# A single-core kernel: the first modulation is loaded first, split into high and low parts, and the preparation of the convolution is moved behind it

## The chip, the core and the metric

The kernel runs on one core of one Trainium2 chip. The metric is the time of one execution on the device in microseconds, lower is better. The median of three runs of the kernel before is 4174.78 us.

## The reference

Two blocks of a sequence model over 1024 tokens of width 1024, batch 1, in float32. What matters here is the start of the first block:

```python
def rmsnorm(x, g):
    xf = x.astype(jnp.float32)
    y = xf * lax.rsqrt(jnp.mean(xf * xf, axis=-1, keepdims=True) + EPS)
    return y.astype(x.dtype) * g

def modulation(cond, w_mod, b_mod):
    m = jax.nn.silu(cond) @ w_mod + b_mod
    return jnp.split(m, 3, axis=-1)
...
    shift, scale, gate = modulation(c[:, None, :], w_mod[i], b_mod[i])
    h = rmsnorm(x, norm_g[i]) * (1 + scale) + shift
    cshift, cscale, cgate = modulation(c_ctx[None, None, :], w_mod[i], b_mod[i])
    hc = rmsnorm(ctx, norm_g[i]) * (1 + cscale) + cshift
    a_val, a_gate, q, k, v, b_gate = jnp.split(h @ w_in, EVEN_SPLITS, axis=-1)
```

`c` and `c_ctx` are two condition vectors of 1024 values, `w_mod[0]` is 1024 x 3072, `ctx` has 256 tokens. Attention, pooling, a second layer with a long convolution (Hyena), Fourier mixing, and then an S5 layer, a stick-breaking attention and two feed-forward layers follow. The long convolution works with spectra of filters that depend on the weights alone: a small sine network over 1024 positions gives hidden units, these give the taps, and the taps are normalized and Fourier transformed. That is the "convolution's preparation" here; its results are not needed before the second layer of the first block.

## The kernel before

Tokens lie along the free dimension and channels on the 128 partitions, in tiles of 128 x 1024 float32 (512 KB, 4 KB on each partition). Large products are made of pairs of tiles in the fp32r type: a high part (a cast on ScalarE) and a low part (the rest, a subtraction on VectorE), with three matmuls for high x high, high x low and low x high (`mm3`, lines 202 to 204; `split`, lines 215 and 216; `weights`, lines 179 to 185, for a panel of weights). Nearly all working tiles come from one pool of 40 slots of 4 KB per partition (`t` and `tr`, tag "t"); weight panels have two slots for the arriving matrix ("wt") and four for its two parts ("wq"); PSUM has two buffers of 1024 columns (`psB`) and four of 512 (`psb`).

The code writes the instructions in one order, and the framework's planner places them into one queue for each engine, by their written order and by when it reckons their operands and slots to be there; an instruction that is free early can so come ahead of what is written before it. On the chip each queue runs in its placed order, and semaphores make an instruction wait for its operands and for its slot. SyncE (SP) issues nearly all loads, GpSimd (POOL) the stores and some copies.

`build` works in this order. `load_consts` loads small constants. `K.hy = Work(K.hy_prep(), 0.6)` makes the preparation of the convolution a generator; a step of it runs up to the next `yield`. `ev_norm` makes the first norm: it runs one step of the preparation, loads x (8 tiles, line 350), runs four more steps (hidden units of the filters, `hy_filters`; tables and the first weights), squares x on ScalarE and sums the squares on VectorE (`sq_acc`, lines 239 to 243), does the same for ctx (`xc`, line 359), and calls `modulation0`.

`modulation0` takes the first 2048 columns of `w_mod[0]` in 16 tiles of 512 KB (`wm`, line 276). Each tile is multiplied in plain float32: the stationary operand is 128 x 2 (the two conditions, `silu_c`), the moving operand half a tile, 512 columns (line 278). After each tile two steps of the preparation are written, 32 in all, so 37 with the five of `ev_norm`. The two rows of results are copied from PSUM (`mrow`, line 285), turned into columns by 16 small matmuls (`pm`, line 288), and give `gain0` and `shift0` (lines 290 to 297). Then `rms_half` makes h in two halves of 512 tokens: column sums (`pc`, line 220), the power -0.5 on GpSimd (`rs_r`, line 228), a broadcast by matmul (`pr`, line 233), and for each of eight tiles one VectorE instruction (`nt`, line 258), the high part on ScalarE (`hh`, line 261) and the low part on VectorE (`hl`, line 262). The same follows for ctx.

`ev_in` is the large input projection: 18 panels of the weights `w_ev` against h (`pbg` gates, `pav`, `pag`, `pq`, `pk`, `pv`); the first two gate panels share the halves, so that they start on the first half of h. Each step over k in `gemm` calls `go()`, 344 calls in all, and `go` issues `rate` steps of the preparation behind each (0.6, that is 206 steps), and 0.1 steps of the other modulations.

The preparation has 5 steps for the hidden units and tables, and 12 spectra of 19 steps: 233. A spectrum (`hy_spectrum`) has 16 matmuls for taps (`pf`, lines 896 and 897), VectorE and ScalarE work on them, a sum over partitions (`pl`, line 918), a row (`pl1r`, line 929), 64 small matmuls as recorded for the transform (`pk`, lines 947 and 948), and 8-point transforms on VectorE, whose results go to DRAM (`khat`, line 955).

Of the kernel before, what the change touches and what calls it, by code (L numbers as in the profile page):

```python
# [35 lines left out]
        ("ln_mix_g_2", 16), ("ln_mix_b_2", 16), ("ln_ffn_g_2", 16), ("ln_ffn_b_2", 16), ("cond", 16))  # L36
# [8 lines left out]
class Work:  # L45
    """instructions that are issued between others, `rate` steps behind each step of a product"""
# [15 lines left out]
class Norm:  # L62
    """layer norm to a (hi, lo) tile per half, and to DRAM; st: the tiles and their sums, set by their product;
    keep: the float32 result replaces the tiles"""
# [39 lines left out]
class Core:  # L104
# [27 lines left out]
    def with_work(self, gen, fg, rate):  # L132
        """runs fg with gen between its products, then the rest of gen"""
        w = Work(gen, rate)
        self.work.insert(0, w)
        fg()
        w.drain()
        self.work.remove(w)

    def lagged(self, tasks):  # L140
        """(product, use) pairs: each use is issued behind the next product"""
# [33 lines left out]
    def weights(self, src, shape, big=False):  # L175
        """a panel of weights as (hi, lo) tiles"""
# [11 lines left out]
    def first4(self, srcs, acts):  # L188
        """four panels, the first half of all before the second; acts: tiles and columns of each half"""
# [55 lines left out]
    def rms_half(self, xs, acc, hv, gain, shift, outs, n=HB):  # L245
        """generator"""
# [19 lines left out]
    def modulation0(self):  # L266
        """shift and scale of block 0, for both conditions"""
# [3 lines left out]
        mod = self.c("mod0", [P, 16, 2])  # L271
        pr = [self.psB("pmr") for _ in range(2)]
        for k in range(KT):
            for c in range(2):
                w = self.t("wm")
                nc.sync.dma_start(w, d["w_mod0"][k, c])
                for hv in HALVES:
                    nc.tensor.matmul(pr[c][:2, hv], self.silu_c[:, 2 * k:2 * k + 2], w[:, hv],
                                     start=k == 0, stop=k == KT - 1)
                for _ in range(2):  # L280
                    next(self.hy.gen)
        rows = [self.t("mrow") for _ in range(2)]
        pm = self.psb("pm")
        for c in range(2):
            nc.scalar.copy(rows[c][:2], pr[c][:2])
            for m in range(KT):
                o = 16 * c + 2 * m
                nc.tensor.matmul(pm[:, o:o + 2], rows[c][:2, m * P:(m + 1) * P], self.ident[:2, :2],
# [10 lines left out]
    def mod_cols(self, src, th, b0, out):  # L299
        """1024 columns of a modulation, for the first condition"""  # L300
# [31 lines left out]
    def halves(hs):  # L332
        """tiles and columns of each half of the tokens"""
# [9 lines left out]
    def ev_norm(self):  # L343
        nc, d = self.nc, self.d
        next(self.hy.gen)
# [6 lines left out]
        for _ in range(4):  # L352
            next(self.hy.gen)
        for k in range(KT):
            for hv in HALVES:
                self.sq_acc(xs[k][:, hv], acc[:, hv], k == 0)
        xc = [self.t("xc", (P, 4, CTX)) for _ in range(2)]
# [5 lines left out]
        self.modulation0()  # L363
        hs = [(self.tr("hh"), self.tr("hl")) for _ in range(KT)]
        for hv in HALVES:
            for _ in self.rms_half(xs, acc[:, hv], hv, self.gain0[:, 0], self.shift0[:, 0],
                                   [(h[:, hv], l[:, hv]) for h, l in hs]):
                pass
# [336 lines left out]
    def out_proj(self, wsrc, acts, evac, order=None, first_half=None, res=None):  # L705
        """first_half: Work, issued along with the second half of the tokens; res: tiles and what they start with"""
# [38 lines left out]
    def hy_filters(self):  # L745
        """hidden units of the filters, [64, L]; the halves of L share the partitions until the end"""
# [50 lines left out]
    def cpair(self, out, a, b, sg):  # L797
        """out[0] = a + sg i b, out[1] = a - sg i b"""
# [7 lines left out]
    def dft8(self, x, sg, sl):  # L806
        """8 point transform of complex [4, 2, 128] tiles, in the orders of T2"""
# [150 lines left out]
    def modulation1(self):  # L958
        """gate of block 0, shift and scale of block 1, gate of block 1"""
# [21 lines left out]
    def hy_natural(self, c, part, c0):  # L981
        """a panel behind its short convolution, in a frame of 128 positions per partition"""
# [1229 lines left out]
```

## Time and profile before

| what | value |
|---|---|
| runs | 4172.21, 4174.78, 4179.71 us; median 4174.78 |
| profiled execution, first to last instruction | 4172.6 us |
| TensorE (PE) busy | 3949.0 us, 95% of the span |
| weight loads (PEld) / VectorE (DVE) / ScalarE (ACT) / GpSimd (POOL) busy | 77% / 68% / 35% / 6% |
| moved by DMA | 449.16 MB, mean 108 GB/s |
| granted TensorE clock, mean | 0.964 |

The profile is one execution; it has no total of its own beside the span of 4172.6 us, which is 2.2 us below the median of the runs. A busy TensorE need not be at its peak, because the ends of matmuls are modelled and because its clock has two levels, 1.2 and 2.4 GHz; the granted clock is given as a share of the higher one. For a row of matmuls the step from one start to the next tells more than the duration of one.

### The profile page before, as it was taken

The numbers are of one execution on the slowest core, as the hardware profiler recorded it, in microseconds if no ns is written. First come the engines' busy times: TensorE is split into PE (matmuls) and PEld (weight loads), VectorE is DVE, ScalarE is ACT, GpSimd is POOL, SyncE is SP. The second block draws the span as 40 slices with busy tenths as digits, with TensorE's granted clock in tenths as the row PEclk, the third lists the DMA queues.
The fourth block names the chain that finished last, engine by engine and source line by source line (L and its number), as shares of the span: only waits on it lengthen the run. The fifth ranks groups of instructions, "written<-read, shape, count | busy, mean of one in ns | idle before, by whom it ended". The sixth has DMA issues, their size and how long they took to land.

```text
span 4172.6 us, 51168 instructions
## 1 busy us (share of the span) xinstructions
PE 3949.0 (95%) x19684; PEld 3206.1 (77%) x19684; DVE 2844.1 (68%) x4892; ACT 1446.3 (35%) x2328; POOL 270.2 (6%) x482
## 2 busy tenths in 40 slices
PE   6899989999999997999999999989999899999997
PEld 3787878777888866787788888768778677888886
DVE  4666667777788968776866664367777867666544
ACT  2222225543121121333433233245555544332332
POOL 0000100022001011000000000010000000000000
PEclk9899999999999998999999999989999899999998
DMA  5333321144122247513322244322222232222542
GB/s 201 107 120 122 116 87 41 36 165 165 66 73 85 74 143 245 174 61 97 131 76 76 91 149 167 108 82 76 61 62 72 75 121 106 76 91 76 174 153 102
DMA packets 169978, 449.16 MB, mean 108 GB/s; under 512 B 37854, under 2 KB 58340, under 8 KB 169734
## 3 DMA queue, kind: packets, MB, share of 16 engines
q1 hardware_dynamic: 129126, 317.94, 23.0%
q0 software_dynamic: 38304, 123.24, 8.5%
q10 hardware_dynamic: 2304, 4.72, 0.4%
q8 instruction: 155, 2.54, 0.2%
q14 instruction: 89, 0.73, 0.1%
HBM read 327.07 MB, written 100.66 MB: 103 GB/s over the span
## 4 chain that ended last, share of the span: by engine, by line
PE 81%; DVE 9%; issue 4%; ACT 3%; DMA 2%; POOL 0%; SPq 0%; ACTq 0%; DVEq 0%; POOLq 0%
PE p L202 7%; PE p L204 7%; PE p L203 7%; PE pd L202 4%; PE pd L204 4%; PE pd L203 4%; PE pout L202 2%; PE pout L204 2%; PE pout L203 2%; DVE sbm L1940 2%; PE pu L202 2%; PE pu L204 2%; PE pu L203 2%; PE pwt L1961 1%; PE pz L1041 1%
## 5 line engine op out<-in xcount | busy, mean ns | idle before, releaser
L185 DVE TENSOR_TENSOR wl<-wt,wh 128x1024 fp32r<-128x1024 f32 x232 | 283.1, 1221 | 335.7 <-ACT wh L184 332.0
L184 ACT CAST wh<-wt 128x1024 fp32r<-128x1024 f32 x232 | 243.0, 1048 | 761.7 <-PE pd L203 213.5
L202 PE MATMUL p<-tq,wq 128*128 128x512 f32 x736 | 292.3, 397 | 3.6 <-ACT wq L215 3.6
L204 PE MATMUL p<-tq,wq 128*128 128x512 f32 x736 | 292.0, 397 | 0.0
L203 PE MATMUL p<-tq,wq 128*128 128x512 f32 x736 | 291.6, 396 | 0.0
L202 PE MATMUL pd<-hd,wh 128*128 128x512 f32 x704 | 278.9, 396 | 0.0
L204 PE MATMUL pd<-hd,wl 128*128 128x512 f32 x704 | 278.7, 396 | 0.0
L203 PE MATMUL pd<-hd,wh 128*128 128x512 f32 x704 | 278.6, 396 | 0.0
L204 PE MATMUL p<-hq,wq 128*128 128x512 f32 x480 | 190.0, 396 | 0.0
L203 PE MATMUL p<-hq,wq 128*128 128x512 f32 x480 | 189.9, 396 | 0.0
L202 PE MATMUL p<-hq,wq 128*128 128x512 f32 x480 | 189.7, 395 | 0.0
L215 ACT CAST wq<-ws 128x512 fp32r<-128x512 f32 x184 | 114.3, 622 | 211.5 <-PE p L204 206.6
L1711 DVE TENSOR_TENSOR fsg<-fsg,p 128x512 f32<-128x512 f32 x140 | 94.3, 686 | 120.1 <-PE p L204 119.9
L202 PEld LDWEIGHTS p<-tq,wq 128*128 128x128 f32 x736 | 138.9, 189 | 43.7 <-ACT wq L215 4.9
L204 PEld LDWEIGHTS p<-tq,wq 128*128 128x128 f32 x736 | 138.8, 189 | 32.4
L203 PEld LDWEIGHTS p<-tq,wq 128*128 128x128 f32 x736 | 139.2, 189 | 31.4
L1711 DVE TENSOR_TENSOR fsu<-fsu,p 128x512 f32<-128x512 f32 x140 | 94.5, 687 | 95.4 <-PE p L204 95.3
L216 DVE TENSOR_TENSOR wq<-ws,wq 128x512 fp32r<-128x512 f32 x184 | 126.6, 689 | 46.8 <-ACT wq L215 44.7
L204 PEld LDWEIGHTS pd<-hd,wl 128*128 128x128 f32 x704 | 132.5, 188 | 31.8
L203 PEld LDWEIGHTS pd<-hd,wh 128*128 128x128 f32 x704 | 132.5, 188 | 31.8
L202 PEld LDWEIGHTS pd<-hd,wh 128*128 128x128 f32 x704 | 132.4, 188 | 31.7
L202 PE MATMUL pu<-hq,wh 128*128 128x512 f32 x320 | 130.0, 406 | 9.4 <-DVE cv L978 9.4
(699 smaller groups left out, 10749.8 us busy)
## 6 DMA issues: line engine op xcount, KB each, us to landing
wt<-w_gu SPq DMA_DIRECT2D x88, 512.0 KB
wt<-w_dn SPq DMA_DIRECT2D x88, 512.0 KB
wm<-w_mod SPq DMA_DIRECT2D x48, 512.0 KB
hid<-fsg POOLq DMA_DIRECT2D x44, 512.0 KB, 4.0
hr<-hid SPq DMA_DIRECT2D x44, 512.0 KB
wt<-w_od SPq DMA_DIRECT2D x28, 512.0 KB
khat<-fX POOLq DMA_DIRECT2D x24, 512.0 KB, 3.0
kh<-khat SPq DMA_DIRECT2D x24, 512.0 KB
```

What stands on the lines that cost most here:

```text
L184: nc.scalar.copy(wh, wt)
L185: nc.vector.tensor_tensor(wl, wt, wh.bitcast(F32), op=ALU.subtract)
L202: mm(ps, lh, rh, start=first, stop=False)
L203: mm(ps, lh, rl, start=False, stop=False)
L204: mm(ps, ll, rh, start=False, stop=last)
L215: self.nc.scalar.copy(h, src)
L216: self.nc.vector.tensor_tensor(l, src, h.bitcast(F32), op=ALU.subtract)
L1041: mm(p4[:, i, q], tb[:, m], z[:, self.POS[m]], start=True, stop=False)
L1711: add = lambda o, u, v: tt(o, u, v, op=ALU.add)
L1940: nc.vector.tensor_tensor_scan(om[:, :n - 1], om[:, :n - 1], self.inv[:, 3:4].to_broadcast([P, n - 1]), 1.0, op0=ALU.mult, op1=ALU.add)
L1961: nc.tensor.transpose(pt[:, s * P:(s + 1) * P], W[x][:, c:c + P], self.ident)
```

## The change

x is loaded first and the tiles of the first modulation right behind it. The constants of `load_consts` and every step of the convolution's preparation come after the first norm: all 233 steps are now issued by `go` within the input projection, at a rate of 0.7 in place of 0.6. ctx is loaded and squared behind the norm of x. The modulation's product is no longer one of plain float32: each tile is split into a high and a low fp32r part, and so are the conditions; the stationary operand is 128 x 128, with high and low parts of the two conditions in its first four columns and zeros in the others (`s4`). The four rows of results are added in pairs by the small matmuls that turn them into columns (a constant `sel` in place of the identity). In the rest of the file only docstrings are left out.

```diff
-        ("ln_mix_g_2", 16), ..., ("cond", 16))
+        ("ln_mix_g_2", 16), ..., ("cond", 16), ("sel", 2))
...
     def modulation0(self):
...
         mod = self.c("mod0", [P, 16, 2])
+        s4 = self.tr("silu4", (P, KT, P))
+        nc.gpsimd.memset(s4.bitcast(F32), 0.0)
+        sc = self.silu_c.rearrange("p (k c) -> p k c", c=2)
+        self.split(sc, s4[:, :, 0:2], s4[:, :, 2:4])
         pr = [self.psB("pmr") for _ in range(2)]
         for k in range(KT):
             for c in range(2):
                 w = self.t("wm")
                 nc.sync.dma_start(w, d["w_mod0"][k, c])
+                wh, wl = self.tr("wmh"), self.tr("wml")
+                self.split(w, wh, wl)
                 for hv in HALVES:
-                    nc.tensor.matmul(pr[c][:2, hv], self.silu_c[:, 2 * k:2 * k + 2], w[:, hv],
-                                     start=k == 0, stop=k == KT - 1)
-                for _ in range(2):
-                    next(self.hy.gen)
+                    nc.tensor.matmul(pr[c][:, hv], s4[:, k], wh[:, hv], start=k == 0, stop=False)
+                    nc.tensor.matmul(pr[c][:, hv], s4[:, k], wl[:, hv], start=False, stop=k == KT - 1)
...
-            nc.scalar.copy(rows[c][:2], pr[c][:2])
+            nc.scalar.copy(rows[c][:4], pr[c][:4])
...
-                nc.tensor.matmul(pm[:, o:o + 2], rows[c][:2, m * P:(m + 1) * P], self.ident[:2, :2],
+                nc.tensor.matmul(pm[:, o:o + 2], rows[c][:4, m * P:(m + 1) * P], self.v("sel", 0, 2)[:4],
...
     def ev_norm(self):
         nc, d = self.nc, self.d
-        next(self.hy.gen)
         xs = []
         acc = self.t("acc")
         for k in range(KT):
             x = self.t("x")
             nc.sync.dma_start(x, d["x_t"][k])
             xs.append(x)
-        for _ in range(4):
-            next(self.hy.gen)
         for k in range(KT):
             for hv in HALVES:
                 self.sq_acc(xs[k][:, hv], acc[:, hv], k == 0)
+        self.modulation0()
+        hs = [(self.tr("hh"), self.tr("hl")) for _ in range(KT)]
+        for hv in HALVES:
+            for _ in self.rms_half(xs, acc[:, hv], hv, ...):
+                pass
         xc = [self.t("xc", (P, 4, CTX)) for _ in range(2)]
         ... (loads and squares of ctx, unchanged)
-        self.modulation0()
-        hs = [(self.tr("hh"), self.tr("hl")) for _ in range(KT)]
-        for hv in HALVES:
-            for _ in self.rms_half(xs, acc[:, hv], hv, ...):
-                pass
...
+               sel=np.tile(np.eye(2), (64, 1)))
...
         K = Core(tc, ctx, d)
+        K.hy = Work(K.hy_prep(), 0.7)
+        hs, hc = K.ev_norm()
         K.load_consts()
-        K.hy = Work(K.hy_prep(), 0.6)
-        hs, hc = K.ev_norm()
         K.side = Work(K.modulation1(), 0.1)
```

## Rows read from the trace of the kernel before

**Rows 1.** Busy time by stage: stretch, length, PE, PEld, DVE, ACT, POOL, clock, DMA share, GB/s.
```profile
0.00:37.00 37.00, 3.97 (x9) 0.67 (x9) 18.64 (x31) 13.46 (x21) 3.60 (x16) 1.00 0.87 310
...
60.00:95.00 35.00, 35.00 (x132) 16.63 (x130) 14.15 (x33) 4.87 (x8) 1.10 (x2) 0.90 0.08 31
...
107.00:591.00 484.00, 465.48 (x2414) 382.42 (x2415) 298.18 (x546) 108.80 (x151) 41.67 (x56) 0.94 0.32 112
```

**Rows 2.** Timeline of TensorE: end of the modulation, first panel (start, length, what).
```profile
93.64 1.02 PE L278 MATMUL pmr<-wm,silu_c 128*2 128x512 f32 x2
...
100.25 3.57 PE L288 MATMUL pm<-ident,mrow 2*128 2x2 f32 x16
...
107.00 1.22 PE L202 MATMUL pbg<-hh,wh 128*128 128x512 f32 x2
...
112.09 0.39 PE L202 MATMUL pbg<-hh,wh 128*128 128x512 f32 x1
112.31 0.39 PE L203 MATMUL pbg<-hl,wh 128*128 128x512 f32 x1
```

**Rows 3.** Timeline of SP's queue, 0 to 420 us.
```profile
0.74 0.39 SPq L121 DMA_DIRECT2D vec<-vecs  x1
...
5.95 3.99 SPq L350 DMA_DIRECT2D x<-x_t  x8
...
13.09 0.33 SPq L849 DMA_DIRECT2D fcos<-dft_fcos  x1
14.37 0.33 SPq L849 DMA_DIRECT2D fnsin<-dft_fnsin  x1
```

**Rows 4.** The chain that ended last, at the loads of x (start, length, what).
```profile
8.49 8.37 DMA x<-x_t
```

**Rows 5.** Timeline of all engines from 0 us: splits of a panel of weights.
```profile
22.64 1.98 ACT L184 CAST wh<-wt 128x1024 fp32r<-128x1024 f32 x2
23.70 2.36 DVE L185 TENSOR_TENSOR wl<-wt,wh 128x1024 fp32r<-128x1024 f32 x2 [2.33 <-ACT wh L184]
```

**Rows 6.** Two shorter stretches, columns as in the first group.
```profile
104.00:110.00 6.00, 5.90 (x20) 4.80 (x21) 5.01 (x12) 2.76 (x4) 0.00 (x0) 0.50 0.00 0
...
120.00:140.00 20.00, 20.00 (x119) 17.40 (x117) 18.95 (x37) 9.99 (x18) 0.70 (x1) 1.00 0.18 63
```

**Rows 7.** Matmuls of 0 to 107 us by line and shape (busy, mean ns | idle).
```profile
L278 PE MATMUL pmr<-wm,silu_c 128*2 128x512 f32 x64 | 32.6, 661 | 0.0
...
L918 PE MATMUL pl<-inv,hacc 128*128 128x1 f32 x16 | 2.1, 253 | 0.0
L770 PE MATMUL ph<-emb,hw 33*64 33x512 f32 x4 | 2.0, 1076 | 5.4 <-DMA hw<-hy_w 5.4
```

**Rows 8.** Timeline of TensorE: steps of the transform and of the taps.
```profile
66.74 0.39 PE L948 MATMUL pk<-hk,fcos 128*128 128x128 f32 x2
66.96 0.39 PE L947 MATMUL pk<-hk,fnsin 128*128 128x128 f32 x2
...
72.67 0.51 PE L896 MATMUL pf<-w3h,hs 128*128 128x256 f32 x1
73.11 0.51 PE L897 MATMUL pf<-w3l,hs 64*128 64x256 f32 x1
```

**Rows 9.** Who waited for whom, TensorE, 107 to 600 us (us, times, longest).
```profile
PE pbg L202 <- ACT bg L461: 9.2, 2, 7.9
```

**Rows 10.** Timeline of ScalarE: what stood ahead of the first gate.
```profile
155.46 1.83 ACT L910 ACTIVATE hab<-hk 128x512 f32<-128x512 f32 x3
157.19 1.00 ACT L461 ACTIVATE bg<-pbg 128x1024 f32<-128x1024 f32 x1
```

**Rows 11.** Who waited for whom, SP, 0 to 130 us.
```profile
SPq L276 <- PE pmr L278: 9.7, 4, 5.7
```

**Rows 12.** Timeline of all engines from 0 us: start and end of the filter chain.
```profile
5.44 1.97 PE L770 MATMUL ph<-emb,hw 33*64 33x512 f32 x4 [5.44 <-DMA hw<-hy_w]
...
36.97 0.58 PE L896 MATMUL pf<-w3h,hs 128*128 128x256 f32 x1 [22.46 <-DMA w3h<-w3h]
```

More of the change, by code (lines that the diff above doesn't have):

```diff
@@ L35 @@
         ("hy_conv_w", 54), ("hy_conv_b", 18), ("final_g", 8),
-        ("ln_mix_g_2", 16), ("ln_mix_b_2", 16), ("ln_ffn_g_2", 16), ("ln_ffn_b_2", 16), ("cond", 16))
+        ("ln_mix_g_2", 16), ("ln_mix_b_2", 16), ("ln_ffn_g_2", 16), ("ln_ffn_b_2", 16), ("cond", 16), ("sel", 2))
 VOFF = {}
@@ L356, in ev_norm @@
                 self.sq_acc(xs[k][:, hv], acc[:, hv], k == 0)
+        self.modulation0()
+        hs = [(self.tr("hh"), self.tr("hl")) for _ in range(KT)]
+        for hv in HALVES:
+            for _ in self.rms_half(xs, acc[:, hv], hv, self.gain0[:, 0], self.shift0[:, 0],
+                                   [(h[:, hv], l[:, hv]) for h, l in hs]):
+                pass
         xc = [self.t("xc", (P, 4, CTX)) for _ in range(2)]
@@ L362, in ev_norm @@
             self.sq_acc(xc[k // 4][:, k % 4], cacc, k == 0, CTX)
-        self.modulation0()
-        hs = [(self.tr("hh"), self.tr("hl")) for _ in range(KT)]
-        for hv in HALVES:
-            for _ in self.rms_half(xs, acc[:, hv], hv, self.gain0[:, 0], self.shift0[:, 0],
-                                   [(h[:, hv], l[:, hv]) for h, l in hs]):
-                pass
         hcH = [self.tr("hcH", (P, 4, CTX)) for _ in range(2)]
@@ L2088, in host @@
                ln_mix_g_2=cols(f["ln_mix_g_2"]), ln_mix_b_2=cols(f["ln_mix_b_2"]),
-               ln_ffn_g_2=cols(f["ln_ffn_g_2"]), ln_ffn_b_2=cols(f["ln_ffn_b_2"]), cond=cond)
+               ln_ffn_g_2=cols(f["ln_ffn_g_2"]), ln_ffn_b_2=cols(f["ln_ffn_b_2"]), cond=cond,
+               sel=np.tile(np.eye(2), (64, 1)))
     a["vecs"] = np.concatenate([src[n] for n, _ in VECS], axis=1)
```

## The prediction

> **What bounds the kernel now.** I read the busy time by stage first. From 107 to 591 us, the input projection, TensorE works 465.5 of 484 us; there the kernel is bound by the matmuls, and only 18.5 us are idle [rows 1]. The first 107 us are different. Up to 37 us TensorE has 4 us of work while the DMA engines are 87% busy: the front waits for loads. From 60 to 95 us it is the other way round: loads are over (8% of the DMA engines) and TensorE is busy in all 35 us, with the modulation and with steps of the convolution's preparation that were written between its tiles. Then the timeline of TensorE: the last product of the modulation starts at 93.64, the first product of the projection at 107.00 [rows 2]. So the projection, the first long stretch that TensorE bounds, starts at 107 us, and before it lies one stretch held by loads and one held by TensorE's own work. The reader is to see that the preparation is useful work wherever it stands: taking it away from the front gives back only what it does not cost again later.
>
> **New start of the projection: the loads.** In the queue of SP x is issued at 5.95 us, behind the small constants; only the vector of constants, issued at 0.74 for 0.39 us, stays ahead of it, so x starts at about 1.2 [rows 3]. A 512 KB tile takes 1.28 us of a saturated queue (the step from one table to the next, 13.09 to 14.37) [rows 3]. The eight tiles of x, issued from 5.95 on, are all there at 8.49 + 8.37 = 16.86, that is 10.9 us later, which is 0.7 + 8 x 1.28 [rows 4]. So the n-th tile lands at 1.9 + 1.28 n. The modulation's 16 tiles stand right behind x: n = 24, 32.6 us. But the planner brings panels of the projection forward: two were cast at 22.64 us, 84 us before their first use [rows 5]. Their slots allow two, and two more once these are split. I count four, n = 28: 37.7 us. The lower bound has none of them, 32.6. What moves behind the modulation is tables, first taps' weights, decay, ctx and constants, 4.2 MB by their shapes, some 10 us of the queue; it then meets a stretch in which the DMA engines are 32% busy [rows 1], so I cost it at nothing. If that cover were missing it would cost those 10 us, through the filter chain below.
>
> **The split and the product.** New per tile: a cast (two start within 1.98 us, 1.0 each) and a subtraction (1.2) [rows 5]. ScalarE has 20 of them, 20 us, VectorE 24 us, beside the squares and sums of x, in 38 us of loading: just enough, so that each keeps up and the last tile is ready 2.2 us after landing, at 39.9. What waits behind a late tile is, on both engines, the next tile, and nobody else. The product was 64 recorded passes, 32.6 us busy [rows 7]. It becomes 64 single passes of 512 columns. A fp32r pass steps by 0.22 us in the first panel at 112 us [rows 2]; the stationary operand grows from 2 to 128 columns, but the panels pay for 128 as well, inside that step. At this pace the last tile adds 0.9: 40.8 us. At the lower clock a pass costs twice that, 0.45, 64 of them 28.8 us, more than the loads supply; counted from the first tile (n = 11, 16.0, split at 18.2) the product ends at 47.0. That TensorE does fall to it the stretch from 104 to 110 us shows: after the small matmuls of one or two columns and a wait for GpSimd it was granted 0.50, that is 1.2 of the 2.4 GHz [rows 6]. I take 44, the middle.
>
> The Trainium skill (TensorE: Matmul & The Clock Gate, on HAM oscillation) says that waits for DMA between bursts of matmuls put the clock back to its lower level before each burst, which speaks against feeding the product tile by tile. By that rule the product ends at 47.0 and the run at about 4151; by the high clock at 40.8 and 4145.
>
> **From the product to the first panel.** The copy of two rows costs 1.0 (as the 1024 columns of a gate do [rows 10]). From the start of the second 16 small matmuls at 100.25 to the first panel at 107.00 were 6.8 us [rows 2]. Together 8. Before, 12.3 us lay between the last product (93.64 + 1.02) and 107.00, since the sums of squares and the power on GpSimd stood in between; now x is summed while the matrix still arrives, so this stands aside. Bounds: 6 (small matmuls at the high clock) and 12.3. The zeros and the split of the conditions happen while x loads. The projection so starts at 44 + 8 = 52, between 32.6 + 3.1 + 6 = 42 and 59, in place of 107: a gain of 55, from 48 to 65.
>
> **What comes back.** 37 steps were done before 107: the hidden units, the first spectrum and 13 of the 19 steps of the second. Their matmuls now stand in the stretch that TensorE bounds: 32 taps at a step of 0.44 [rows 8], 14.1; 64 passes of one transform, two in 0.22 [rows 8], 7.1; the filters' two layers, 2.0 each [rows 7], 4.0; the sums over partitions, 2.1 [rows 7]; two rows, 0.7. Sum 28, from 25 (some under a wait) to 30 (some at the lower clock). The rate of 0.7 gives 240 steps in 344 calls, enough for 233; before, 206 were enough for the remaining 196. So the preparation ends as late in the projection as before. Its VectorE and ScalarE work goes along; VectorE is at 298 of 484 us [rows 1]. ctx behind x costs nothing while the keys that need it are hundreds of microseconds away.
>
> **Waits inside the projection.** Of the 18.5 idle us 9.2 are two waits for a gate [rows 9]: TensorE waited 7.9 us for a PSUM buffer whose evacuation, at 157.19, stood on ScalarE behind absolute values of taps [rows 10]. The third panel still needs a buffer of the first two, and steps of a spectrum are still mixed in, though other ones. I leave it at that, with -9 (this wait gone) to +10 (one more like it).
>
> **Sum.** 4172.6 - 55 + 28 = 4145.6 for the profiled execution. The median of the runs before is 2.2 above it, so 4148. With the ends of all terms: 4174.8 - 65 + 25 - 9 = 4126 to 4174.8 - 48 + 30 + 10 = 4167.
>
> **Rivals.** *The moved work is hidden.* If the preparation fills the 18.5 us of waits in the projection, only 28 - 18.5 = 9.5 come back: 4174.8 - 55 + 9.5 = 4129. For it: the waits exist [rows 9]. Against: the steps are placed between products by count, and the longest wait came from such steps [rows 10]. Chance 0.08.
>
> *The tiles take turns*, so the change loads first but not faster. Each tile now needs three slots, and slots come back only behind the split and the product. Before, SP already waited four times, 9.7 us, for a slot behind a product [rows 11]. If only two tiles are in flight, a trip of 2.0 (load) + 2.2 (split) + 1.3 (product), 5.5, gives one tile in 2.75 in place of 1.28: 16 x 1.47 = 24 us later, a start at 76, 4174.8 - 31 + 28 = 4172. Against: some 30 of the 40 slots are free at that time, ten tiles. Chance 0.10.
>
> *The filter chain is exposed*, and the kernel becomes slower. From the first layer of the hidden units at 5.44 to the first taps at 36.97 were 31.5 us, nearly all of it under the loads [rows 12]. Now the chain starts with the projection, and its VectorE steps compete with making h, when VectorE is busy 18.95 of 20 us [rows 6]; that stretch of 22 us can be added: 53. By the written order the taps stand behind eight calls, 24 products, 5.5 us into the projection. If TensorE's queue keeps that order it stands for 53 - 5.5 = 48 us: 4148 + 48 = 4196. Beyond 27 us of such waiting the gain is gone, beyond 35 the kernel is slower. Against: at 36.97 the taps ran ahead of the product that was written before them (45 us and later), so the planner places by readiness, and two panels, 96 products or 22 us, need nothing from the chain. Chance 0.08.
>
> **How the numbers follow.** The forecast has 0.74. A measurement of this kernel tells about 0.2%, 8.3 us, from no change: faster means under 4166.4, slower over 4183.1. Faster: 0.72 of the forecast, the hidden case 0.08 and the better part of the turns 0.03, 0.83. Same: 0.10, most of the turns. Slower: 0.07, the exposed chain. The range from 4128 to 4168 holds nearly all of the forecast, the upper part of the hidden case and a little of the turns.
>
> **What would show it.** Right: the modulation's loads end near 38 us, its products near 44, the first panel's product starts near 52; the projection then lasts about 28 us longer than 484; everything behind is moved by 27. Wrong: loads of the modulation that wait for slots, gaps of more than 2 us between its tiles, TensorE waiting for taps or for their copies early in the projection, or a projection that lasts much more or less than 512 us.

## The result and the profile after

| | before | after |
|---|---|---|
| runs, median (lowest to highest) | 4174.83 (4172.21 to 4179.71, 4 runs) | 4210.69 (4209.86 to 4215.99, 4 runs) |
| ratio of the runs, 95% interval | | 1.0086 [1.0072, 1.010] |
| profiled execution, span | 4172.6 | 4214.2 |
| first product of the projection | 107.0 | 62.2 |
| first attention score | 591.2 | 627.6 |
| projection, between the two | 484.2 | 565.4 |

The kernel became 0.86% slower, some 36 us; 4148 with a range from 4128 to 4168 was forecast. In the profiled executions 36.4 of 41.6 us are lost by the first score, and the 5 us behind it are within what single executions differ by (that stretch took 3574 to 3592 us in the profiles here whose spectra all end ahead of the scores, five runs apart that have a gain of their own, told at h2).

TensorE alone, before and then after, by stretch (ends, length, busy, granted clock, DMA share, GB/s); the 107 to 591 us of [rows 1] in pieces like those of after:

```profile
0.00:107.00 107.00, 72.43 (x245) 0.92 0.54 196
107.00:151.00 44.00, 43.39 (x192) 0.85 0.17 60
151.00:240.00 89.00, 78.87 (x375) 0.90 0.44 148
240.00:480.00 240.00, 237.15 (x1186) 0.96 0.33 112
480.00:591.20 111.20, 106.26 (x666) 0.94 0.30 105
```

```profile
0.00:62.20 62.20, 33.42 (x128) 0.93 0.69 259
62.20:87.40 25.20, 25.17 (x96) 0.89 0.00 0
87.40:151.10 63.70, 33.58 (x124) 0.61 0.41 134
151.10:240.00 88.90, 83.84 (x393) 0.90 0.38 132
240.00:480.00 240.00, 236.19 (x1155) 0.94 0.32 110
480.00:627.60 147.60, 132.36 (x770) 0.86 0.24 86
```

Take length minus busy. Up to the first score TensorE was idle for 53.1 us before (34.6 in the front, 18.5 in the projection) and for 83.1 after (28.8 and 54.3). The sum of busy time is 538.1 against 544.6. So of the 44.8 us by which the projection starts earlier, 39.0 are work that left the front and only 5.8 are idle time saved; and the projection got 45.5 us of work and 35.8 of idle time, 30 of that from 87.4 to 151.1. That stretch on TensorE, lines of its timeline:

```profile
87.02 0.40 PE L204 MATMUL pbg<-hh,wl 128*128 128x512 f32 x1
90.00 0.58 PE L220 MATMUL pc<-inv,cacc 128*128 128x1 f32 x4 [2.59 <-DVE cacc L243]
...
97.88 1.97 PE L771 MATMUL ph<-emb,hw 33*64 33x512 f32 x4 [5.05 <-DMA emb<-hy_emb]
105.05 1.97 PE L773 MATMUL ph<-hd,hw 64*64 64x512 f32 x4 [5.20 <-ACT hd L781]
119.08 0.58 PE L897 MATMUL pf<-w3h,hs 128*128 128x256 f32 x1 [12.06 <-DMA w3h<-w3h]
...
129.92 1.84 PE L919 MATMUL pl<-inv,hacc 128*128 128x1 f32 x8 [2.27 <-DVE hacc L913]
132.01 0.59 PE L930 MATMUL pl1r<-ident,rn 128*1 128x128 f32 x2 [0.25 <-DVE rn L923]
134.28 0.77 PE L948 MATMUL pk<-hk,fcos 128*128 128x128 f32 x2 [1.68 <-issue]
...
151.08 0.79 PE L202 MATMUL pbg<-hh,wh 128*128 128x512 f32 x1
```

Two gate panels are done at 87.4. The third needs a PSUM buffer of theirs, and instead the whole chain of the filters runs: hidden units, taps, sum, first transform, one behind the other. The end of the wait stands on ScalarE:

```profile
112.16 0.62 ACT L215 CAST hsl<-hd 128x512 fp32r<-128x512 f32 x1
112.69 1.04 ACT L215 CAST w3h<-w 64x1024 fp32r<-64x1024 f32 x1
122.02 0.63 ACT L911 ACTIVATE hacc<-hk 128x512 f32<-128x512 f32 x1 [8.29 <-DVE hk L909]
...
140.55 0.59 ACT L795 COPY ev<-pk 128x512 f32<-128x512 f32 x1 [11.50 <-PE pk L949]
144.12 0.59 ACT L795 COPY ev<-pk 128x512 f32<-128x512 f32 x1 [2.99 <-PE pk L949]
144.60 1.03 ACT L462 ACTIVATE bg<-pbg 128x1024 f32<-128x1024 f32 x1
```

`bg` reads a panel that was done 57 us earlier, but it is placed behind the last copy of the first spectrum. This is the wait of [rows 10], which had 7.9 us before: there the chain had run under the loads [rows 12], here it starts at 97.88. And why so late? The queue of SP, and its longest wait (us, times, longest):

```profile
5.32 0.44 SPq L280 DMA_DIRECT2D wm<-w_mod  x1
...
16.17 0.43 SPq L280 DMA_DIRECT2D wm<-w_mod  x1
21.69 1.46 SPq L179 DMA_DIRECT2D wt<-w_ev  x2
23.20 13.19 SPq L280 DMA_DIRECT2D wm<-w_mod  x14
...
47.67 0.43 SPq L880 DMA_DIRECT2D skip<-hy_skip  x1
87.69 2.20 SPq L179 DMA_DIRECT2D wt<-w_ev  x2
...
90.94 0.33 SPq L750 DMA_DIRECT2D emb<-hy_emb  x1
```

```profile
SPq L179 <- DVE cacc L243: 41.6, 2, 39.8
```

The row names the instruction of VectorE that came last; the slot itself came free with the split of a third panel on VectorE, which had to wait for the first two panels to be used:

```profile
86.44 1.23 DVE L185 TENSOR_TENSOR wl<-wt,wh 128x1024 fp32r<-128x1024 f32 x1 [2.09 <-ACT wh L184]
```

So from 48 to 87.7 us SP waits for slots of two weight panels, and everything behind them, the filters' first input `emb` and all tables, waits along, while the DMA engines have nothing to do (share 0.00 from 62 to 87).

### The profile page after: what moved, and what is told of

It is laid out like the page before. It is cut to its first block, busy times and chain, and to the rows that moved or that the text cites. A ratio compares the mean times of both kernels' runs of the same rounds, so it can differ in the third digit from the quotient of the medians.

```text
span 4214.2 us, 51219 instructions
## 1 busy us (share of the span) xinstructions
PE 3959.8 (94%) x19684; PEld 3226.2 (77%) x19684; DVE 2866.7 (68%) x4909; ACT 1465.2 (35%) x2345; POOL 270.8 (6%) x483
## 4 chain that ended last, share of the span: by engine, by line
PE 78%; DVE 11%; issue 4%; ACT 3%; DMA 3%; SPq 1%; POOL 0%; DVEq 0%; ACTq 0%; POOLq 0%
PE p L203 7%; PE p L202 7%; PE p L204 7%; PE pd L202 4%; PE pd L204 4%; PE pd L203 4%; PE pout L202 2%; PE pout L204 2%; PE pout L203 2%; DVE sbm L1941 2%; PE pu L202 2%; PE pu L204 2%; PE pu L203 2%; PE pwt L1962 1%; PE pk L948 1%
## 5 line engine op out<-in xcount | busy, mean ns | idle before, releaser
L204 PEld LDWEIGHTS p<-tq,wq 128*128 128x128 f32 x736 | 138.6, 188 | 32.6
L203 PEld LDWEIGHTS p<-tq,wq 128*128 128x128 f32 x736 | 138.9, 189 | 31.5
L216 DVE TENSOR_TENSOR wq<-ws,wq 128x512 fp32r<-128x512 f32 x184 | 126.7, 690 | 46.8 <-ACT wq L215 44.5
L215 ACT CAST wq<-wt 128x512 fp32r<-128x512 f32 x138 | 85.5, 619 | 150.8 <-PE p L204 145.2
```

What stands on the lines that cost most here:

```text
L203: mm(ps, lh, rl, start=False, stop=False)
L204: mm(ps, ll, rh, start=False, stop=last)
L215: self.nc.scalar.copy(h, src)
L216: self.nc.vector.tensor_tensor(l, src, h.bitcast(F32), op=ALU.subtract)
```

## The experiments

Sixteen more kernels were run, in five groups. "Plain" means that the modulation's product is that of the kernel before, no split.

**First group: which part of the change costs?** e1 and e2 each change one thing in the changed kernel, e3 undoes the split, e4 does the split alone in the kernel before.

```diff
e1_claim:       +        sg2 = [self.t("bg") for _ in range(2)]
                +        for sg in sg2:
                +            nc.vector.memset(sg[:, 0:1], 0.0)
                ...
                -                sg = self.t("bg")
                +                sg = sg2[h] if h < 2 else self.t("bg")
e2_chain_early: +        for _ in range(4):
                +            next(self.hy.gen)
                         self.modulation0()
e3_plain:       modulation0's product and its rows as before, all else as changed
e4_split_only:  the kernel before with the changed modulation0's product
```

e1. 

> The changed kernel, but the two tiles into which the first two gates are evacuated are claimed from the pool, by a one-column memset, before the first panel, so that they do not stand behind the slots of the preparation in written order. Theory A (the first evacuations wait in the planned order behind the filter chain and the first spectrum, because slots are handed out as written, and both PSUM buffers stay full from 87 to 145 us): the gates are evacuated at about 88 us, the third panel's products start before 100 us, the idle time of TensorE between 87 and 151 us falls from 30 us to under 10, and the time is 20 to 35 us under the changed kernel, about 4180. Rival B (TensorE's own queue holds the taps ahead of the panels, whatever the evacuation does): products of the third panel still start near 150 us and the time stays within 8 us of 4211. Rival C (the stall moves on to the third and fourth gate): the third panel starts early, but a stall of 20 us or more stands before the fifth, and less than 15 us are gained.

e2. 

> The changed kernel, but the four steps that make the hidden units of the filters are written behind the squares of x and ahead of the modulation, as before the change; tables, first weights and all spectra stay behind. Theory A (the filter chain, 91 to 113 us, is exposed and holds the first gates): the first taps run at about 97 in place of 119 us, and the time is about 20 us under the changed kernel, 4190. Rival D (the stall is set by the first spectrum, its tables and its slots, not by the hidden units): the first taps stay later than 110 us and the time stays within 8 us of 4211. If the small loads and four copies of the chain delay the modulation's tiles, the first panel starts later than 62 us by as much.

e3. 

> The changed kernel with the plain float32 product of before in place of the split one; the order of loads and of the preparation stays as changed. Theory E (the split is what keeps the product at the pace of the loads): the product, 64 passes of 0.43 us at the high clock or 0.85 at the low one, ends 5 to 30 us later than 55 us, and the time is 5 to 30 us above the changed kernel. Rival F (the loads set the pace, and the split costs order: tiles for its parts are handed out in written order, so that small loads and panel loads get between the modulation's loads): the first panel starts at 62 us or earlier and the time is equal to the changed kernel or up to 10 us lower.

e4. 

> The kernel before with the split product alone; the order of loads and the preparation stay as before. Theory E: TensorE was busy from 60 to 95 us with passes of the modulation among other work; 64 passes get shorter by 0.2 us, so the first panel starts about 13 us earlier, near 94, and the time is about 13 us under before, 4162. Rival G: the casts and subtractions, 17 and 19 us more on ScalarE and VectorE, and three slots for each tile slow the front by as much; within 6 us of before, or slower.

Measured: e1 1.0088 [1.0059, 1.0116], e2 1.0059 [1.0038, 1.008], e3 1.0062 [1.0039, 1.0084], e4 0.9993 [0.9982, 1.0004]. So the split alone changes nothing (though e4's first panel came at 113.2, not near 94), and without it the change still loses 0.6%: most of the loss is in the move. In e1 the first two gates were read out at 97.2, ahead of the taps, and the wait came back at the next pair of panels (ScalarE):

```profile
97.22 1.92 ACT L465 ACTIVATE bg<-pbg 128x1024 f32<-128x1024 f32 x2
...
183.45 0.59 ACT L798 COPY ev<-pk 128x512 f32<-128x512 f32 x1 [2.99 <-PE pk L952]
183.93 1.03 ACT L465 ACTIVATE bg<-pbg 128x1024 f32<-128x1024 f32 x1
```

Panels three and four ran from 98.27 to 126.7, and then the next gate stood behind two spectra. Giving the first read-outs their place only shifts the stall. In e2 the first panel came later, at 72.8, and the taps stayed at 120.3, now waiting for `w3h`, whose weights were still loaded behind SP's long wait (until 97.4), and the first gate at 144.1. Who waited for whom (us, times, longest):

```profile
PE pf L899 <- DMA w3h<-w3h: 17.8, 1, 17.8
```

So four of the five steps ahead of the spectra are not enough. e3 started the projection at 56.2, 6 us before the split product let it.

**Second group: move the chain away.**

```diff
f1_later:        -        K.work = [K.hy, K.side]
                 +        K.work = [K.side]
                 ...      (behind the first two gate panels, and at a rate of 0.76)
                 +        self.work.insert(0, self.hy)
f2_loads_first:  +        ws = [self.t("wm") for _ in range(2 * KT)]
                 +        (all 16 loads of the matrix, ahead of the first split)
f3_chain_hidden: e2 + e3 + f1
f4_tables_early: f3, and
                          self.modulation0()
                 +        next(self.hy.gen)      (tables, w3, decay)
```

f1. 

> The changed kernel with no preparation step among the first two gate panels; the steps start behind them, at 0.76 steps per step of the projection where it was 0.70. Theory (the chain from the hidden units to the taps and the first spectrum has to run somewhere in the projection, and the panel written behind it waits): the first panels are read out before the chain, the third panel starts near 90 us and not at 151, but the stall comes back behind panel four or five, and the score product starts at 615 to 630 us: 4200 to 4215 us. Rival (the place of the first two read-outs was the whole loss): the stall of 30 us goes, the score product starts near 597 us, 4180 us or less.

f2. 

> The changed kernel with the loads of all sixteen tiles of the first modulation matrix written ahead of their splits. Theory (the splits and the second weight panel in the order of loads cost the front some 6 to 10 us, as the plain product's earlier first panel showed): the first panel starts at 52 to 57 us instead of 62; the chain of the preparation, not the front, sets when panel three starts, so it stays near 150 us and the time within 5 us of the changed kernel's 4211. Rival (the late front is passed on in full): 4201 us.

f3. 

> The plain product, the four steps of the hidden units written ahead of the first modulation, and the preparation's other steps only behind the first two gate panels. Theory (the loss is the time in which the hidden units, the taps and the first spectrum run one after the other inside the projection): the first panel starts at 57 to 65 us, there is no stretch in the first 100 us of the projection with over 10 us without a product, the projection takes 510 to 525 us in place of 565, the score product starts at 570 to 590 us, before the 591 of the kernel before: 4155 to 4175 us, faster than before. Rival (the loss is the moved work and the lower clock, 46 us of products, and goes with the order of the projection whatever hides the chain): the projection stays above 540 us and the time at 4190 us or more.

f4. 

> As the run with the hidden units ahead of the modulation, and the step that loads the tables and the filters' last weights directly behind the modulation matrix too, ahead of the context and the third weight panel. Theory (a chain that waits for a load in the queue of SP is exposed as much as one that computes): the taps start 10 us or more earlier than in the run beside it, and the time is 0 to 10 us less than its. Rival (taps are not what anything waits for once the hidden units are early, and the tables only push the context and weights back): the first panel 3 to 5 us later and the time 3 to 10 us more than the run beside it.

Measured: f1 1.0088 [1.0059, 1.0117], f2 1.010 [1.0063, 1.0136], f3 1.0056 [1.0034, 1.0078], f4 1.0036 [1.0022, 1.0049]. f1 went as the theory said: first gate at 99.4, stall later, nothing won. f2 missed: all loads of the matrix were issued by 24.9 us, yet the first panel started at 64.7 instead of 52 to 57. ScalarE's queue shows why (us, times, longest):

```profile
ACT wh L184 <- DMA wt<-w_ev: 13.8, 1, 13.8
```

The casts of two weight panels stand among the splits of the tiles; with the panels now loaded behind the matrix, the tiles that had arrived waited for them. f3 missed its size: no wait over 7.1 us was left in the first 100 us of the projection, but the start was late, at 72.4, and the projection took 553 us, not 510 to 525. Here the hidden units' inputs were loaded behind x, and TensorE stood 15.9 and 8.5 us for them ahead of the modulation. f4's taps start at 105.0 in place of 123.6, and it won another 11 us at the median (the intervals overlap), though its first panel came at 79.0; its idle time up to the first score is 66.6 us against 74.1 in f3.

**Third group: is it the order of loads?** These three start from the kernel before and leave all 37 steps ahead of the projection.

```diff
g1_matrix_before_x: (hidden units, tables, then)
                    +        pr = self.modulation0a()    loads, products, 2 steps a tile
                             x = self.t("x") ...
g2_matrix_spread:   as g1; the four steps ahead of it spread, 3 a tile for the first four
g3_prep_in_product: x, ctx, then the product with all 37 steps between its tiles
```

g1. 

> The kernel before with one move: x and the context are loaded behind the modulation matrix, not ahead of the preparation's tables and the matrix; the 37 preparation steps stay where they were, ahead of the first panel, and the product stays plain. Theory (TensorE has the same work ahead of the score product whatever the order, so that only its idle time counts: 34.6 us in the front before, 22.5 of it in the wait for the filters' last weights, which stood behind x in the queue): the taps start at 24 to 28 us in place of 37, the first panel 8 to 13 us before 107, the projection keeps its 484 us and 18 us of idle time, the score product starts at 578 to 584 us: 4160 to 4168 us, faster than before. Rival (the statistics of x, now last to arrive, take the place of the wait): the first panel at 105 to 115 us and 4173 to 4183 us.

g2. 

> As the run beside it, and the first tiles of the matrix ahead of the tables too, with three preparation steps behind each of the first four tiles. Theory (idle time of the front is what counts): products of the matrix fill the wait for the hidden units, but the tables and the filters' weights come two tiles, 2.6 us, later; the first panel within 3 us of the run beside it and the time within 5 us of it. Rival (an early product is worth its length, 2 tiles of 4 products, 3.7 us): 4 us less than the run beside it.

g3. 

> The kernel before with x, the context and the first tile of the modulation matrix ahead of everything of the preparation, whose 37 steps all stay between the tiles of the plain product, ahead of the first panel. So the matrix and x are first, as in the change, but nothing moves into the projection. Theory (the loss comes from preparation moved into the projection, and what stays in the front costs only what its chain is late, 8 to 12 us): the first panel at 112 to 120 us, the projection 475 to 490 us, 4175 to 4187 us. Rival (x and the matrix first is itself what costs, by the later tables and panels of weights): 4200 us or more.

Measured: g1 1.0001 [0.9989, 1.0014], g2 1.000 [0.9988, 1.0012], g3 1.0021 [1.0005, 1.0036]. g3 came out as the theory had it: first panel at 118.0, projection 481.9 us, 4183.9 us. Loading x and the matrix first costs 0.2% as long as nothing moves into the projection. g1 and g2 refuted a hope, not the theory: the taps came 2 us earlier in g1, at 35.2, and not 10, in g2 later, at 38.5, and the squares of x, now last on ScalarE, held back the copy of the product's rows (TensorE waited 4.7 us for it); the first panel came at 108.9 and 109.9, and g1's front has 36.6 us of idle time, 2 more than before.

**Fourth group: the rate, and the chain ahead of x.** By now the prediction's error had a place, but f4 still lacked 15 us on the kernel before.

```diff
h1_rate:             -K.hy_prep(), 0.7)    +K.hy_prep(), 0.95)      (changed kernel, split kept)
h2_chain_early:      f4, but the first step of the preparation ahead of the loads of x,
                     three steps ahead of the squares of x
h3_chain_early_rate: h2 with a rate of 0.95
```

h1. 

> The changed kernel with the preparation's rate at 0.95 steps per step of the projection, where it was 0.70, so that it ends before the context's keys and values and not among them. Theory (besides the stall of the first 90 us, the changed kernel loses 15 us of idle time from 480 to 628 us, where the last spectra are issued beside short products that cannot cover their chains): third panel still near 150 us, idle time behind 480 us down to 5 us, 4195 to 4204 us. Rival (the waits behind 480 us come wherever the last spectra are placed): within 5 us of the changed kernel's 4211.

h2. 

> As the run with the tables behind the modulation matrix, but the hidden units' loads stand ahead of x as in the kernel before, and their steps ahead of the squares of x, so that TensorE doesn't stand 24 us for them ahead of the modulation. Theory (idle time counts wherever it stands): the hidden units are done at 13 to 16 us, the plain products of the modulation end at 47 to 50 us, the first panel starts at 57 to 63 us instead of 79, the projection keeps the 544 us of that run: 4170 to 4180 us. Rival (a start earlier by 16 to 22 us only makes the first panels wait for the tables, the taps or ScalarE): 4187 us or more.

h3. 

> As the run beside it, with the rate of 0.95. Theory: the idle time behind 480 us goes too, 8 to 12 us less than the run beside it, 4160 to 4170 us, faster than the kernel before. Rival (more steps between the gate panels delay their read-outs): no gain on the run beside it, or 3 to 8 us more.

Measured: h1 1.0104 [1.0077, 1.0131], h2 1.0007 [0.9994, 1.002], h3 1.0044 [1.0027, 1.006]. h1 did what it was to do late in the projection, 4.3 us idle from 480 to the first score in place of 15.2, and lost more before that:

```profile
240.00:360.00 120.00, 111.07 (x530) 0.90 0.28 94
360.00:480.00 120.00, 111.10 (x510) 0.86 0.25 91
480.00:560.00 80.00, 79.79 (x428) 1.00 0.34 112
```

(columns as above; 17.8 us idle from 240 to 480, 3.8 in the changed kernel.) More steps between two products mean more waits, so the theory of a tail that costs by itself is refuted; h3, 18 us above h2 where 8 to 12 us below were expected, says the same. h2 has the hidden units done under the loads again and no stall; TensorE's timeline of its front:

```profile
3.91 1.97 PE L770 MATMUL ph<-emb,hw 33*64 33x512 f32 x4 [3.91 <-DMA hw<-hy_w]
11.07 1.97 PE L772 MATMUL ph<-hd,hw 64*64 64x512 f32 x4 [5.18 <-ACT hd L780]
22.30 30.46 PE L278 MATMUL pmr<-wm,silu_c 128*2 128x512 f32 x64 [9.27 <-DMA wm<-w_mod]
...
71.00 0.77 PE L202 MATMUL pbg<-hh,wh 128*128 128x512 f32 x1
```

It starts the projection 36 us before the kernel before did (though not at 57 to 63, as expected) and takes the same time as that (4178.7 against 4175.0). The projection is 541.5 us, 57 more than before, with 32.5 us idle and 509.0 busy. So by the first score the profiled h2 is still 21.3 us late (612.5), and 15.1 us ahead of the changed kernel.

Part of what it gains behind that lies far from what the change touches. From the first `pd` product (a feed-forward layer, 2459 us before) to the end, six runs take 1702.9 to 1704.5 us: e2, f3, f4, h2, h3 and i1. All the others and the kernel before take 1711.7 to 1715.4. The 2112 recorded `pd` products are busy for 829.8 to 830.7 us in these six and for 835.3 to 836.2 elsewhere; a third of them, before and then in h2 (busy, mean ns | idle):

```profile
L202 PE MATMUL pd<-hd,wh 128*128 128x512 f32 x704 | 278.9, 396 | 0.0
```

```profile
L202 PE MATMUL pd<-hd,wh 128*128 128x512 f32 x704 | 276.9, 393 | 0.0
```

These six, and no other run, have the first steps of the preparation written ahead of `load_consts`. Why later products are then faster is open, but some 10 us of each of their gains lie there.

**Fifth group: where else could the moved steps go?**

```diff
i1_early_then_scores:  h2 at a rate of 0.60;  i2_before_then_scores: the kernel before at 0.50; both:
-        K.hy.drain()
         K.side.drain()
...
+        K.hy.rate = 1.7
+        K.work = [K.side, K.hy]
         y = K.ev_attn(ks, vs, scls)
+        K.hy.drain()
```

i1. 

> As the run with the hidden units ahead of x, with the rate back at the 0.60 of the kernel before (it was 0.76 there, 0.70 in the change), and the some 40 preparation steps that are then left spread over the score units behind the projection, 1.7 to each. Theory (what costs is the density of preparation steps between the products, since their chains on VectorE and ScalarE are not covered by so few products; the score units leave TensorE 34 us of idle time from 591 to 900): the score product starts at 565 to 580 us, the units behind it take 20 to 30 us longer, 4160 to 4172 us, faster than before. Rival (the steps cost their products and their chains wherever they stand): 4178 us or more, no gain.

i2. 

> The kernel before with the rate at 0.50 in place of 0.60, and the some 34 steps left over on the score units, 1.7 to each: the same move without any other order of loads. Theory: the projection is 30 to 40 us shorter, the score units 15 to 30 us longer, 4160 to 4172 us. Rival (steps cost the same in both places): 4175 us within 5.

Measured: i1 0.9984 [0.997, 0.9998], i2 1.0062 [1.004, 1.0083]. The two stretches, projection and then the score units to the last score product, in i1 and i2:

```profile
71.20:561.60 490.40, 467.82 (x2344) 0.90 0.31 108
561.60:873.60 312.00, 275.71 (x1803) 0.97 0.12 42
```

```profile
108.20:592.90 484.70, 464.28 (x2293) 0.89 0.32 109
592.90:889.90 297.00, 262.37 (x1749) 0.98 0.12 45
```

Before, the score units took 268.2 us, 239.5 busy. In i2 they took 29 us more, 23 of it work, and the projection was not shorter, though it had 123 recorded matmuls fewer: its granted clock was 0.89 in place of 0.94. So neither theory held there: the steps cost more at the scores than they had in the projection. i1 pays 44 us at the scores and wins 29.6 by the first score: its profiled span is that of before, since the stretch behind the scores took 14 us less, 10 of them behind the first `pd` product, as in the five other runs named at h2; the ratio is 0.16% lower. It is the only version whose interval lies below the kernel before, by less than the 0.2% that a measurement here can tell, and these 10 us are more than its whole gain.

**All in one table**, us, from the profiled executions: length and idle time of front and projection, and their idle time together.

| run | front | idle | projection | idle | idle, both | ratio |
|---|---|---|---|---|---|---|
| before | 107.0 | 34.6 | 484.2 | 18.5 | 53.1 | 1 |
| after | 62.2 | 28.8 | 565.4 | 54.3 | 83.1 | 1.0086 |
| e1 | 60.6 | 28.8 | 569.8 | 51.6 | 80.4 | 1.0088 |
| e2 | 72.8 | 36.3 | 558.9 | 46.4 | 82.7 | 1.0059 |
| e3 plain | 56.2 | 17.0 | 565.3 | 54.4 | 71.4 | 1.0062 |
| e4 split only | 113.2 | 44.5 | 474.5 | 17.2 | 61.7 | 0.9993 |
| f1 | 63.3 | 29.2 | 573.2 | 47.9 | 77.1 | 1.0088 |
| f2 | 64.7 | 33.6 | 563.5 | 54.5 | 88.1 | 1.0100 |
| f3 | 72.4 | 29.4 | 553.4 | 44.8 | 74.1 | 1.0056 |
| f4 | 79.0 | 34.3 | 543.6 | 32.3 | 66.6 | 1.0036 |
| g1 | 108.9 | 36.6 | 491.0 | 19.0 | 55.6 | 1.0001 |
| g2 | 109.9 | 32.6 | 481.9 | 19.1 | 51.7 | 1.0000 |
| g3 | 118.0 | 46.4 | 481.9 | 18.7 | 65.1 | 1.0021 |
| h1 | 60.7 | 29.2 | 576.6 | 58.1 | 87.3 | 1.0104 |
| h2 | 71.0 | 24.5 | 541.5 | 32.5 | 57.0 | 1.0007 |
| h3 | 69.2 | 24.3 | 560.2 | 43.5 | 67.8 | 1.0044 |
| i1 | 71.2 | 24.7 | 490.4 | 22.6 | 47.3 | 0.9984 |
| i2 | 108.2 | 35.6 | 484.7 | 20.4 | 56.0 | 1.0062 |

In the eleven rows with the steps in the projection (after, e1 to e3, f1 to f4, h1 to h3), the ratio goes by the idle time, wherever that stands, once the 10 us of the feed-forward layers are added back to e2, f3, f4, h2 and h3: from some 13 us lost at 57.0 us of idle time (h2) to 42 at 88.1 (f2). These two numbers are estimates from the ratios and the profiles. Work counts beside it: e4, with less of it on TensorE, 526 us in place of 538, stands apart, and i1 and i2 have part of it behind the projection. No row shows an early first panel as a gain of its own.

## Why the prediction was wrong

**The step that failed** is "The third panel still needs a buffer of the first two, and steps of a spectrum are still mixed in, though other ones. I leave it at that". What is mixed in there is the head of the chain, and the wait of [rows 9] did not stay at 7.9 us: 30 us of idle time lie between panels two and three. The chain of [rows 12] had been costed at 31.5 us, in a rival that got 0.08, and its cover, the loads, had been named. The sign was right there (forecast 4196, measured 4211), the mechanism only in part. TensorE's queue was not in the way as such, and two panels did run without the chain, as the argument against the rival said. But the first read-out of a gate was placed behind the first spectrum on ScalarE, and the chain's first product came 36 us behind the start of the projection, because SP waited for a slot. A second term that was put at nothing failed with it: the loads behind the modulation were to meet DMA engines that have time, which they had (share 0.00), but the queue that issues them stood still for 39.8 us. The runs show both: e1 moved the read-outs alone and the stall came back one pair of panels later; e2 moved the hidden units alone and the taps still waited for loads; h2 hid all of the chain's head, and the projection had 32.5 us of idle time in place of 54.3. By the runs h2 got 33 of the 36 us back, but not all through this: some 10 lie in the feed-forward layers, and up to 10 may belong to the plain product (e3, 1.0062 against 1.0086, intervals that overlap). No run moved the loads alone.

**Start of the projection: 52 forecast, 62.2 measured**, a gain of 44.8 and outside the 48 to 65 given. Of the 16 tiles the second was issued at 16.17 and the other 14 from 23.20 on, since constants, four weight panels and a wait for their slots came in between. The cast of the last one started at 46.29; it was to land at 37.7. The product did not end at 44 either; its last three passes, of the last tile, run at 53.77 to 55.4, behind small matmuls of the modulation's rows and of the norm (TensorE):

```profile
53.77 0.77 PE L285 MATMUL pmr<-wml,silu 128*128 128x512 f32 x1
```

The two paces of the estimate both occur: the first passes step by 0.43 us, those from 36.85 on by 0.235. The Trainium skill (TensorE: Matmul & The Clock Gate, on HAM oscillation) tells of waits for DMA between bursts that are long enough for each burst to start at the lower clock; the prediction had taken it for any such wait. The pace of the burst at 30.73, behind a wait of 5.1 us, agrees, though the granted clock reads 1.00 there; the waits between tiles from 37 to 48 us were under 0.3 us, passes kept the step of 0.235, and they are no test of it.

**What comes back: 28 forecast, 45.5 measured** as busy time of the projection. The instructions are those that were counted: 32 more taps, 64 more passes of a transform, the two layers and the sums are recorded there. What the sum had only as an upper end ("some at the lower clock") is a lower granted clock over the projection: 0.87 in place of 0.94. In the stall it is 0.61, and there, up to 139.1, the first transform's passes step by 0.43 per two in place of 0.22 [rows 8]; behind the stall it is 0.91. The stall is not the only cause, since h2 and f4 have 0.88 without it; what else lowers it is open, since i2, with fewer steps mixed in than before, had 0.89 too. How much of the 17.5 us the clock explains was not separated.

**The sum** with measured terms, to the first score: -44.8 + 45.5 + 35.8 = +36.5, against -55 + 28 + 0 = -27.

**Other rivals.** "The moved work is hidden" is refuted: in every run with all steps in the projection its idle time rose above the 18.5 us of before (least in f4, 32.3). "The tiles take turns" did not happen as stated, as SP's longest single wait at the matrix's loads was 1.4 us; the tiles were late for the other reasons above.

**Settled and open.** That the move of the preparation carries most of the loss, and not the split or the order of the loads, is shown by e4, g3 and e3. That its exposed head and the read-outs behind it are the larger part of the added idle time is shown by f4 and h2: with the head hidden, 22 of the 35.8 us are gone. They are not the larger part of the projection's growth: of 81 us h2 took 24 back. Why the preparation costs as much in the projection as the front saves, even with its head hidden, is shown only as far as the numbers go: TensorE is busy 94% of the projection in h2 and 96% before, so moved work adds its own length, and a low clock is added to it. Open is also why the feed-forward layers are 10 us faster in six runs.

The Trainium skill (Perfetto Trace Analysis, Optimization Strategy) says that a kernel whose most contended engine changes over time may gain by interleaving the stretches. The kernel before did that in its front, the preparation under the loads; the change took it apart, and the 5.8 us of idle time it saved there against 35.8 added agree with the rule.

## What to carry to other kernels

Before moving work out of a stretch that looks idle, subtract its busy time from its length: here 72 of 107 us of the front were work that had to be done somewhere, and only the idle 35 could be won. Work whose first results come from a long chain of loads and small steps belongs under a stretch that waits for other loads; moved beside dense products it holds what is written behind it, because each engine's queue, the loads' too, runs in its placed order. After a read-out is moved ahead, look at the next one: a stall between buffers is not gone until the chain it stands behind is. And read a variant's gain in the stretch that it changes, not in the total alone: here 10 us of six totals lay far behind the change.

## What the runs showed of the hardware

The granted clock and the pace of the passes can disagree in one stretch. In the changed kernel the profile gives 1.00 for 30.0 to 36.4 us, where a pass of 512 columns steps by 0.43 us, and 1.00 again for 36.9 to 45.0, where it steps by 0.23:

```profile
30.00:36.40 6.40, 5.20 (x11) 1.00 1.03 417
36.90:45.00 8.10, 7.76 (x31) 1.00 0.98 393
```

```profile
35.57 0.63 PE L285 MATMUL pmr<-wml,silu 128*128 128x512 f32 x1
36.00 0.63 PE L284 MATMUL pmr<-wmh,silu 128*128 128x512 f32 x1
...
37.32 0.40 PE L284 MATMUL pmr<-wmh,silu 128*128 128x512 f32 x1
37.56 0.39 PE L285 MATMUL pmr<-wml,silu 128*128 128x512 f32 x1
```

And the plain product of 64 recorded passes took 30.5 us in one row in h2, where it ran without other work in between, against 32.2 busy for the split one; in e4 the split one took 35.0 (17.4 and 17.6), where the plain one took 32.6 before. In these runs splitting the tiles saved TensorE nothing.
